# A second anchor for the first weight split of the GLU: ScalarE's half of it is ordered behind the last copy of the S5 loop's outputs

## The chip, the cores and the metric

The kernel runs on one core of a Trainium2 chip. The metric is device time in microseconds (us) of one execution. The core's engines are TensorE (PE in the profile, its weight loads PEld), VectorE (DVE), ScalarE (ACT), GpSimd (POOL) and SyncE (SP, which issues the DMAs). Each runs its own instructions in the order in which they were laid out, and waits on semaphores for the others.

## The reference, cut to what matters

Two layers of a residual network over 256 tokens of width 1024, then a second block. The place of interest is the mixer of the second layer: a bidirectional state-space recurrence (S5), a GELU, and a gated linear unit (GLU) with two 1024x1024 weight matrices.

```python
def _mixer_s5(h, lam_re, ..., d_skip, w_glu_a, w_glu_b):
    ...
    y = lax.map(one_sequence, ug).reshape(bsz, seq, dm)      # the S5 recurrence, both directions
    y = (y + d_skip.astype(f32) * u).astype(h.dtype)
    z = jax.nn.gelu(y)
    return (z @ w_glu_a) * jax.nn.sigmoid(z @ w_glu_b)
```

After it come the layer's feed-forward part, and a second block with three kinds of attention and a gated feed-forward part, nearly all of it dense products with float32 weights.

## The kernel before, in words

**Dense products.** A float32 weight tile of 1 MB is loaded by one DMA (`load`, L298) into one of four `w` buffers and split in four pieces by `hilo`: ScalarE writes the high part of a piece (`hi`, L314, 128x512), VectorE the rest (`lo`, L315). `mm3` (L319 to L321) then makes three matmuls for each block of 128: high weights by high activations, high weights by low activations, low weights by high activations. The same `hilo` splits activations.

**The S5 loop** (`s5`) runs over eight steps `ip`. In each, `chunk_states` multiplies the inputs by a table `Wt` on TensorE, ScalarE copies the result out of PSUM (the copy of `X`, L1047), TensorE transposes it (L1051), and `scan` works on it on VectorE: two products (L1064, L1065), a sum and a difference (L1066, L1067), the recurrence (L1068) and two products (L1072, L1073); GpSimd joins these into `S` (L1075, L1076). `outputs` multiplies the inputs by `Mt` (L1087) and `S` by `Vt` (L1089) into PSUM. Of every second step ScalarE copies the outputs to `Y` (L1122); the last of the four such copies is that of step 7. `chunk_states` runs one step ahead of `scan`. `X`, `S` and the two inputs of GpSimd share a ring of five buffers.

**The tail.** `finish(0)` and `finish(1)` handle the two halves of the channels. Each transposes its half of `Y` (L1099), adds the skip term on VectorE (L1102, eight instructions), takes the GELU on ScalarE (L1103) and splits the result in `z` high (L314) and low (L315), four pieces each. `finish(0)` needs only the steps 0 to 3, and its VectorE instructions are held behind the scan of step 7; `finish(1)` needs the last copy of `Y`.

**The GLU** (`j` = 0 to 3) loads and splits one tile of each matrix (`Wa`, `Wb`) and runs 48 matmuls for each, the even blocks first, which need only `finish(0)`, then the odd ones, which need `finish(1)`. Ahead of it `between` starts the preparation of the memory input `m` (squares L155, split L1230 and L1231); its ScalarE instructions are held behind the last one of `finish(1)`.

**What sets the order.** A planner lays the instructions of each engine out before the run, by the order of the code and by its own estimate of when inputs are ready; extra edges (`add_manual_dep`, set by `held` and `held_at`) tie it: an instruction that is emitted inside such a block is laid out behind the named one on its engine. `scanned` is such a set of anchors. It is made in each step and, after the loop, holds VectorE's last instruction of the scan of step 7. The split of the first GLU tiles (`j == 0`) is emitted inside `held_at(scanned)`, so VectorE's `lo` pieces come behind that scan. ScalarE's `hi` pieces and the loads have no anchor.

Of the kernel before, what the change touches and what calls it, by code (L numbers as in the profile page):

```python
# [174 lines left out]
class K:  # L175
# [784 lines left out]
    def s5(self, x, u, fill, need, between, each, l=1):  # L960
# [57 lines left out]
        def load(ip):  # L1018
            Wt = wide("Wt", self.wplace[ip], ip)
            Wt = [w.rearrange("p (e r d q) -> p e r d q", e=4, r=2, d=2) for w in Wt]  # L1020
            dm = tab([128, 2, 8, 32], "dm")
            if ip % 2 == 0:

                mt.append(room("Mt", self.mplace[ip // 2]).rearrange("p (a i e n) -> p a i e n", a=2, i=2, e=4))
                src = self.Kd[ip // 2]
                for s in range(8):
                    nc.sync.dma_start(mt[-1][16 * s:16 * s + 16].rearrange("c a i e n -> c (a i e) n"),
                                      bass.AP(tensor=src.tensor, offset=src.offset + 16 * s, ap=[[240, 16], [3840, 16], [1, 128]]))
            Mt = mt[-1][:, ip % 2]
            Et = self.E[:, :, 8 * ip:8 * ip + 8]  # L1030
            nc.gpsimd.memset(dm[:, :, :, 0], 0.0)
            (nc.scalar.copy if self.dm_act else nc.gpsimd.tensor_copy)(dm[:, :, :, 1:], self.rho[:, None, 8 * ip:8 * ip + 8, None].to_broadcast([128, 2, 8, 31]))
            Vt = wide("Vt", self.vplace[ip], ip)
            Vt = [w.rearrange("p (e r n) -> p e r n", e=4, r=2) for w in Vt]
            return Wt, Vt, Mt, Et[:, 0], Et[:, 1], dm

        def chunk_states(ip, tabs):

            Wt = tabs[0]
            pX = self.ps("mm").rearrange("p (i r d q) -> p i r d q", i=2, r=2, d=2)  # L1040
            for i in range(2):
                for d in range(2):
                    for e in range(4):
                        lhs = Ur[:, 2 * ip + i, e] if d else U[:, 2 * ip + i, 32 * e:32 * e + 32]
                        nc.tensor.matmul(pX[32 * e:32 * e + 32, i, :, d], lhs, Wt[i][:, e, :, d], start=True, stop=True, tile_position=(0, 32 * e))
            X = self.sb([128, 2, 2, 128])
            nc.scalar.copy(X, pX.rearrange("p i r d q -> p i r (d q)"))  # L1047
            pT = self.ps().rearrange("p (r i x) -> p r i x", r=2, i=2)
            for r in range(2):
                for i in range(2):  # L1050
                    nc.tensor.transpose(pT[:, r, i], X[:, i, r], self.ident)  # L1051
            return pT.rearrange("p r i (e j) -> p r (i e) j", e=4)
# [5 lines left out]
        def scan(pT, tabs):  # L1058
            cs, sn, dm = tabs[3:]
            both = lambda a: a[:, None].to_broadcast([128, 2] + list(a.shape[1:]))  # L1060

            t = [self.sb([128, 2, 8, 32], tag="q2") for _ in range(2)]
            a, b = t[0][:, :, :, 1:], t[1][:, :, :, 1:]
            tt(a, pT[:, :, :, 0:31], both(cs[:, :, 1:]), op=ALU.mult)  # L1064
            tt(b, pT[:, ::-1, :, 0:31], both(sn[:, :, 1:]), op=ALU.mult)  # L1065
            tt(Z[:, 0, :, 1:], a[:, 0], b[:, 0], op=ALU.add)  # L1066
            tt(Z[:, 1, :, 1:], a[:, 1], b[:, 1], op=ALU.subtract)  # L1067
            v.tensor_tensor_scan(fl(Tt), fl(dm), fl(Z), 0.0, op0=ALU.mult, op1=ALU.add)  # L1068
            S = self.sb([128, 2, 8, 32])
            fw, bw = slice(0, 64), slice(64, 128)  # L1070
            t = [self.sb([128, 2, 8, 32]) for _ in range(2)]
            tt(t[0], Tt, both(cs), op=ALU.mult)  # L1072
            tt(t[1], Tt[:, ::-1], both(sn), op=ALU.mult)  # L1073
            for r, op in ((0, ALU.subtract), (1, ALU.add)):
                nc.gpsimd.tensor_tensor(S[fw, r], t[0][fw, r], t[1][fw, r], op=op)  # L1075
                nc.gpsimd.tensor_tensor(S[bw, r, :, ::-1], t[0][bw, r], t[1][bw, r], op=op)  # L1076
            return S

        def outputs(ip, S, tabs, pY):
            _, Vt, Mt = tabs[:3]  # L1080
            for i in range(2):
                for k in range(3):
                    for e in range(4):
                        o = pY[32 * e:32 * e + 32, 2 * (ip % 2) + i]
                        kw = dict(start=k == 0, stop=k == 2, tile_position=(0, 32 * e))
                        if k == 0:
                            nc.tensor.matmul(o, U[:, 2 * ip + i, 32 * e:32 * e + 32], Mt[:, i, e], **kw)  # L1087
                        else:
                            nc.tensor.matmul(o, S[:, k - 1, 4 * i + e], Vt[i][:, e, k - 1], **kw)  # L1089

        def finish(ih):
            if ih == 0:
                z.extend(self.sb([128, 8, T], F32R, "h") for _ in range(2))
            zh, zl = z
            for t2 in range(2):
                po = self.ps("mm").rearrange("p (t e j) -> p t e j", t=4, e=4)
                for t in range(4):
                    src = Y[:, 4 * t2 + t, 8 * ih:8 * ih + 8].rearrange("p i c -> p (i c)")
                    nc.tensor.transpose(po[:, t].rearrange("p e j -> p (e j)"), src, self.ident)  # L1099
                for e in range(4):  # L1100
                    ut = u[:, ih, 4 * t2:4 * t2 + 4, e]
                    v.scalar_tensor_tensor(ut, ut, self.col("s5_d", 2 * e + ih), po[:, :, e], op0=ALU.mult, op1=ALU.add)  # L1102
            nc.scalar.activation(u[:, ih], u[:, ih], AF.Gelu_apprx_tanh)  # L1103
            for e in range(4):
                self.hilo(zh[:, 2 * e + ih].rearrange("p (t j) -> p t j", t=8), zl[:, 2 * e + ih].rearrange("p (t j) -> p t j", t=8), u[:, ih, :, e])
# [5 lines left out]
        for ip in range(8):  # L1111
            if ip + self.ahead < 8:
                tabs[ip + self.ahead] = load(ip + self.ahead)
            if ip + self.skew < 8:
                pT[ip + self.skew] = chunk_states(ip + self.skew, tabs[ip + self.skew])
            S = scan(pT.pop(ip), tabs[ip])
            scanned = {mybir.EngineType.DVE: self.last(mybir.EngineType.DVE)}
            if ip % 2 == 0:
                pY = self.ps(self.y_tag[ip // 2 % 2]).rearrange("p (i n) -> p i n", i=4)
            outputs(ip, S, tabs.pop(ip), pY)  # L1120
            if ip % 2:
                nc.scalar.copy(Y[:, :, 2 * ip - 2:2 * ip + 2].rearrange("p t i c -> p i t c"), pY.rearrange("p i (t c) -> p i t c", c=16))  # L1122
            if ip == 3 + self.defer:
                with self.held(mybir.EngineType.DVE):
                    finish(0)
            self.behind(fill, self.rates[2][1])
# [589 lines left out]
```

## Time and profile before

| | us |
|---|---|
| median of three runs | 1231.25 (1230.14 to 1233.12) |
| the profiled execution's own time | 1230.7 |
| its span on the core | 1228.9 |
| TensorE busy in the span | 1164.5 (95%) |
| VectorE busy | 888.7 (72%) |
| ScalarE busy | 610.8 (50%) |
| GpSimd busy | 97.4 (8%) |

The busy times are sums over stages with different limits; what ends last in a stage is read from its timeline. The times below are microseconds from the start of the span. TensorE's granted clock is a share of its full speed: 1.00 is 2.4 GHz, 0.50 is 1.2 GHz, and a value between is a mixture of the two within the stretch.

### The profile page before, as it was taken

The numbers are of one execution on the slowest core, as the hardware profiler recorded it, in microseconds if no ns is written. First come the engines' busy times: TensorE is split into PE (matmuls) and PEld (weight loads), VectorE is DVE, ScalarE is ACT, GpSimd is POOL, SyncE is SP. The second block draws the span as 40 slices with busy tenths as digits, with TensorE's granted clock in tenths as the row PEclk, the third lists the DMA queues.
The fourth block names the chain that finished last, engine by engine and source line by source line (L and its number), as shares of the span: only waits on it lengthen the run. The fifth ranks groups of instructions, "written<-read, shape, count | busy, mean of one in ns | idle before, by whom it ended". The sixth has DMA issues, their size and how long they took to land. (4 is left out here: it accounts for less than half of the span.)

```text
span 1228.9 us, 25406 instructions
## 1 busy us (share of the span) xinstructions
PE 1164.5 (95%) x10482; PEld 1104.8 (90%) x10482; DVE 888.7 (72%) x1827; ACT 610.8 (50%) x1202; POOL 97.4 (8%) x132
## 2 busy tenths in 40 slices
PE   5899898999999965899999999999999999999998
PEld 3698688999999953799999999999999999999998
DVE  7879888898989776857755656686666686665564
ACT  3577346555555542445544545563465545554441
POOL 0077310000000024200000000000000000000000
PEclk9799999999999976899999999999999999999999
DMA  9889786797988999354566655452444444555541
GB/s 341 326 315 331 300 319 203 242 308 276 312 290 273 272 279 294 142 174 169 176 240 217 225 176 181 151 175 101 144 166 138 167 167 151 194 180 177 193 154 60
DMA packets 69980, 267.29 MB, mean 218 GB/s; under 512 B 7381, under 2 KB 35429, under 8 KB 43241
## 3 DMA queue, kind: packets, MB, share of 16 engines
q1 hardware_dynamic: 69864, 265.68, 63.3%
q8 instruction: 82, 1.34, 0.4%
q14 instruction: 34, 0.27, 0.1%
HBM read 246.85 MB, written 18.81 MB: 216 GB/s over the span
## 5 line engine op out<-in xcount | busy, mean ns | idle before, releaser
L315 DVE TENSOR_TENSOR lo<-w,hi 128x512 fp32r<-128x512 f32 (+1 forms) x640 | 421.7, 702 | 142.5 <-ACT hi L314 142.0
L314 ACT ACTIVATE hi<-w 128x512 fp32r<-128x512 f32 (+1 forms) x640 | 358.1, 625 | 333.1 <-PE mm L320 117.4
L319 PE MATMUL mm<-h,hi 128*128 128x256 f32 x1328 | 381.5, 288 | 0.9 <-ACT hi L314 0.4
L321 PE MATMUL mm<-h,lo 128*128 128x256 f32 x1328 | 379.6, 286 | 0.1
L320 PE MATMUL mm<-h,hi 128*128 128x256 f32 x1328 | 378.6, 285 | 0.2 <-DVE h L384 0.2
L319 PEld LDWEIGHTS mm<-h,hi 128*128 128x128 f32 x1328 | 255.9, 193 | 8.7 <-issue 3.6
L321 PEld LDWEIGHTS mm<-h,lo 128*128 128x128 f32 x1328 | 255.8, 193 | 2.8 <-issue 1.5
L320 PEld LDWEIGHTS mm<-h,hi 128*128 128x128 f32 x1328 | 255.9, 193 | 1.3 <-issue 0.7
L320 PE MATMUL at<-s,hi 128*128 128x256 f32 x720 | 204.4, 284 | 0.0
L319 PE MATMUL at<-s,hi 128*128 128x256 f32 x720 | 204.4, 284 | 0.0
L321 PE MATMUL at<-s,lo 128*128 128x256 f32 x720 | 203.9, 284 | 0.0
L319 PEld LDWEIGHTS at<-s,hi 128*128 128x128 f32 x720 | 138.0, 192 | 1.8 <-issue 1.4
L320 PEld LDWEIGHTS at<-s,hi 128*128 128x128 f32 x720 | 138.0, 192 | 0.6 <-issue 0.6
L321 PEld LDWEIGHTS at<-s,lo 128*128 128x128 f32 x720 | 137.8, 192 | 0.4 <-issue 0.4
L443 PE MATMUL fa<-wa,crep 128*32 128x256 f32 x704 | 53.0, 418 | 8.0 <-DMA wa<-in_ada_dram 4.5
L541 POOL TENSOR_TENSOR s<-s,cv 128x256 f32<-128x256 f32 x60 | 50.1, 871 | 39.7 <-ACT cv L540 39.6
L443 PEld LDWEIGHTS fa<-wa,crep 128*32 128x32 f32 x704 | 20.7, 116 | 27.2 <-DMA wa<-in_ada_dram 6.7
L320 PE MATMUL fp<-h,hi 128*128 128x256 f32 x144 | 40.9, 284 | 1.6 <-DVE h L315 1.6
L319 PE MATMUL fp<-h,hi 128*128 128x256 f32 x144 | 40.8, 284 | 0.0
L321 PE MATMUL fp<-h,lo 128*128 128x256 f32 x144 | 40.7, 283 | 0.0
L540 ACT ACTIVATE cv<-ap,s 128x256 f32<-128x256 f32 x60 | 29.5, 505 | 17.4 <-POOL s L541 16.6
L937 ACT COPY Wt<-fp 128x512 f32<-128x512 f32 x32 | 18.6, 581 | 34.6 <-PE fp L936 28.0
(438 smaller groups left out, 1814.0 us busy)
## 6 DMA issues: line engine op xcount, KB each, us to landing
w<-in_fc_dram SPq DMA_DIRECT2D x64, 1024.0 KB, 5.1
wa<-in_ada_dram SPq DMA_DIRECT2D x44, 1024.0 KB, 6.5
w<-in_w_in_dram SPq DMA_DIRECT2D x38, 1024.0 KB, 4.9
w<-in_w_gate_dram SPq DMA_DIRECT2D x11, 1024.0 KB, 5.0
w<-in_w_up_dram SPq DMA_DIRECT2D x11, 1024.0 KB, 4.9
Vd<-V SPq DMA_DIRECT2D x16, 512.0 KB, 5.4
w<-in_w_out_dram SPq DMA_DIRECT2D x8, 1024.0 KB, 5.8
Wd<-Wt SPq DMA_DIRECT2D x16, 512.0 KB, 5.7
```

The costliest lines, as they stand in the source:

```text
L314: self.nc.scalar.activation(hi, h, AF.Copy)
L315: self.nc.vector.tensor_tensor(lo, h, hi.bitcast(F32), op=ALU.subtract)
L319: mm(ps, sh, mh, start=start, stop=False, skip_group_check=True)
L320: mm(ps, sh, ml, start=False, stop=False, skip_group_check=True)
L321: mm(ps, sl, mh, start=False, stop=stop, skip_group_check=True)
L443: nc.tensor.matmul(ps[32 * q:32 * q + 32], self.crep[:, 2 * k + k2], w[:, n:n + 256], start=k == 0 and k2 == 0, stop=k == 3 and k2 == 1, t ...
L540: nc.scalar.mul(t, src, w)
L541: nc.gpsimd.tensor_tensor(acc[:, ch], acc[:, ch], t, op=ALU.add)
L937: nc.scalar.copy(W[:, :, k], pt.rearrange("p (e x) -> p e x", e=4))
```

## The change

After the copy of `Y` in a step, the set of anchors gets a second entry: ScalarE's last instruction, which is that copy. At the end of the loop `scanned` so holds VectorE's last instruction of the scan and ScalarE's last copy of `Y`. The eight `hi` pieces of the first two GLU tiles are therefore laid out behind the last copy of `Y`. No instruction is added or removed, and no other edge changes.

```diff
             outputs(ip, S, tabs.pop(ip), pY)
             if ip % 2:
                 nc.scalar.copy(Y[:, :, 2 * ip - 2:2 * ip + 2].rearrange("p t i c -> p i t c"), pY.rearrange("p i (t c) -> p i t c", c=16))
+                scanned[mybir.EngineType.Activation] = self.last(mybir.EngineType.Activation)
             if ip == 3 + self.defer:
                 with self.held(mybir.EngineType.DVE):
                     finish(0)
```

## Rows read from the trace of the kernel before

**Rows 1.** Windows: stretch, length, busy us (instructions) per engine, granted clock, DMA share, GB/s

```profile
465.00:470.00 5.00, 4.92 (x76) 3.95 (x80) 2.68 (x5) 1.58 (x3) 0.15 (x2) 0.50 1.04 411
485.00:490.00 5.00, 0.00 (x0) 0.00 (x0) 0.00 (x0) 1.46 (x3) 0.00 (x0) 0.50 0.74 306
505.00:510.00 5.00, 3.38 (x28) 3.15 (x27) 4.93 (x15) 0.03 (x1) 0.00 (x0) 1.00 0.97 357
...
600.00:650.00 50.00, 50.00 (x421) 50.00 (x420) 31.33 (x53) 23.78 (x44) 0.00 (x0) 1.00 0.59 211
```

**Rows 2.** Waits of TensorE from 507 us on: total us, times, longest

```profile
PE fp L320 <- DVE h L315: 1.6, 1, 1.6
PE mm L320 <- DVE h L384: 0.2, 1, 0.2
```

**Rows 3.** Timeline of ScalarE: start, us, line, operation, [idle before <- releaser]

```profile
488.54 2.19 ACT L314 ACTIVATE hi<-w 128x512 fp32r<-128x512 f32 x4 [9.91 <-DMA w<-in_glu_b_dram]
490.64 0.56 ACT L1047 COPY s<-mm 128x512 f32<-128x512 f32 x1
491.10 2.19 ACT L314 ACTIVATE hi<-w 128x512 fp32r<-128x512 f32 x4
495.70 0.59 ACT L1122 COPY s<-at 128x512 f32<-128x512 f32 x1 [2.41 <-PE at L1089]
500.87 1.06 ACT L1103 ACTIVATE s<-s 128x1024 f32<-128x1024 f32 x1 [4.58 <-DVE s L1102]
501.95 1.33 ACT L314 ACTIVATE h<-s 128x256 fp32r<-128x256 f32 x4
503.56 0.59 ACT L1122 COPY s<-at 128x512 f32<-128x512 f32 x1 [0.27 <-PE at L1089]
509.97 1.06 ACT L1103 ACTIVATE s<-s 128x1024 f32<-128x1024 f32 x1 [5.82 <-DVE s L1102]
...
512.30 1.14 ACT L155 ACTIVATE q<-m 128x512 f32<-128x512 f32 x2
...
517.58 2.17 ACT L314 ACTIVATE hi<-w 128x512 fp32r<-128x512 f32 x4
```

**Rows 4.** Timeline of VectorE around the last scan and in the tail

```profile
481.56 1.23 DVE L1068 TENSOR_TENSOR_SCAN fp<-dm,fa 128x512 f32<-128x512 f32 x1
492.41 0.67 DVE L1064 TENSOR_TENSOR q<-at,E 128x496 f32<-128x496 f32 x1 [9.61 <-PE at L1051]
...
498.69 2.15 DVE L1102 SCALAR_TENSOR_TENSOR s<-s,vec,mm 128x128 f32<-128x128 f32 x8
500.75 5.77 DVE L315 TENSOR_TENSOR lo<-w,hi 128x512 fp32r<-128x512 f32 x8
506.44 1.42 DVE L315 TENSOR_TENSOR h<-s,h 128x256 fp32r<-128x256 f32 x4
507.79 2.14 DVE L1102 SCALAR_TENSOR_TENSOR s<-s,vec,mm 128x128 f32<-128x128 f32 x8
511.50 1.43 DVE L315 TENSOR_TENSOR h<-s,h 128x256 fp32r<-128x256 f32 x4 [1.57 <-ACT h L314]
```

**Rows 5.** Timeline of TensorE: end of step 7's chunk states, the hole, the GLU's start

```profile
473.34 0.27 PE L1045 MATMUL mm<-Wt,s 128*32 128x128 f32 x1
...
480.91 0.46 PE L1087 MATMUL at<-Vt,s 128*32 128x128 f32 x4 [0.81 <-issue]
491.25 1.12 PE L1051 MATMUL at<-ident,s 128*128 128x128 f32 x4 [9.88 <-ACT s L1047]
...
506.91 0.39 PE L320 MATMUL fp<-h,hi 128*128 128x256 f32 x1 [1.62 <-DVE h L315]
```

**Rows 6.** Timeline of GpSimd and of SyncE's queue: the issues that matter

```profile
478.03 0.73 POOL L1076 TENSOR_TENSOR s<-s,s 64x256 f32<-64x256 f32 x1
...
477.18 0.30 SPq L1027 DMA_DIRECT2D Mt<-Kd  x1
...
478.50 1.36 SPq L298 DMA_DIRECT2D w<-in_glu_a_dram  x1
```

**Rows 7.** DMA issues of narrow windows: size, us from issue to landing

```profile
Mt<-Kd SPq DMA_DIRECT2D x1, 128.0 KB, 6.5
...
w<-in_glu_a_dram SPq DMA_DIRECT2D x1, 1024.0 KB, 9.9
```

## The prediction

> **What bounds the kernel now.** I read the windows first, to find where TensorE is not full; then TensorE's waits behind the S5 loop; then the timelines of ScalarE, VectorE and TensorE between 473 and 518 us; last the landings of the transfers. In the windows the reader should see that from the GLU on TensorE has no hole: a stretch of 50 us holds 421 matmuls and is busy throughout [rows 1], and from 507 us to the end it waits on other engines twice, for 1.6 and 0.2 us [rows 2]. So whatever brings that stream forward brings the end forward, us for us, as long as the stream stays closed. The stream begins at 506.91, when the second GLU matmul gets its low activations [rows 5]. Ahead of it lies a hole: between 485 and 490 us TensorE, VectorE and GpSimd do nothing at all [rows 1].
>
> The timelines say whose hole it is. VectorE ends the recurrence of step 6 at 481.56 + 1.23 = 482.79 and then stands for 9.61 us until TensorE has transposed X of step 7; TensorE stands 9.88 us for ScalarE's copy of that X [rows 4, 5]. The product that the copy reads was done at 473.6 [rows 5]. The copy came at 490.64, because four `hi` pieces of the first GLU tile stood ahead of it on ScalarE, and these waited 9.91 us, from 478.63 on, for their weights [rows 3]. The tile was issued at 478.50 and took 9.9 us to land: 488.4, and the pieces start at 488.54 [rows 3, 6, 7]. The row names the other tile as the releaser, but this landing is the one that fits.
>
> **The change part by part.** Nothing is added or removed. Eight `hi` pieces move on ScalarE from either side of the copy of X of step 7 to behind the last copy of `Y`. Loads, SyncE and GpSimd keep their order.
>
> *The loop.* Without the pieces, X of step 7 still needs a buffer of the ring of five, which GpSimd frees when it ends `S` of step 4: 478.03 + 0.73 = 478.76 [rows 6]. With 0.56 us for the copy it is there at 479.4. TensorE is free at 480.91 + 0.46 = 481.37, and four transposes take at most 1.12, the figure at the low clock [rows 5]: 482.5 at the latest. VectorE is busy until 482.79. So its 9.61 us go, whole, and the rest of the loop moves up by 9.6 us.
>
> What is late next in the loop is the table `Mt` of steps 6 and 7: its last part is issued at 477.18 and lands 6.5 us later, at 483.7 [rows 6, 7]. TensorE's matmuls on it stand right behind the transposes, so TensorE waits about 1.2 us there with the outputs of step 5 queued behind. The copy of those outputs (495.70, so 486.1 when shifted) feeds only `finish(1)` [rows 3], and VectorE does not wait for it; I cost it at nothing. If the planner lays the `Mt` matmuls ahead of the transposes instead, VectorE waits until 483.7 + 0.6 + 1.1, some 2.6 us: that is the price if the cover is gone.
>
> *The tail.* Here the pieces now cost something. All of it 9.6 us earlier: the GELU of half 0 at 491.3, its high parts until 493.7, the last copy of `Y` from 493.96 to 494.55 [rows 3]. Then come the eight `hi` pieces, at 2.19/4 = 0.55 us each [rows 3]: until about 498.9. VectorE cannot start on the `lo` pieces at 491.2 as a mere shift of 500.75 would have it, but at about 495.1. It can use the gap for the low parts of half 0 (1.42 us, 492.9 to 494.3), which now stood behind the eight `lo` pieces. From 495.1 it has 5.77 (`lo`) + 2.14 (skip term of half 1) + 1.43 (low parts of half 1) = 9.34 us of work [rows 4], and is through at 504.5 at the earliest; shifted alone it would have been through at 511.50 + 1.43 - 9.6 = 503.3. So the tail gives back about 1.2 us.
>
> How this reaches TensorE depends on an order that the trace of before cannot show; I bound it from both sides. At 50/421 = 0.119 us per matmul [rows 1] the 96 matmuls of `j` = 0 take 11.4 us, 5.7 for the even blocks. Before, the odd blocks could start at 506.91 + 5.7 = 512.6, or 503.0 shifted. Worse end: VectorE makes all eight `lo` pieces first (to 500.9), then the skip term (503.0); GELU 1.06 and a first high part bring 504.5, and a first low part 504.8 [rows 3, 4]: 1.8 us late. Better end: the skip term first, as soon as the transposes of half 1 are done. Then the `lo` pieces come last, at 504.5, with only the last two blocks of one tile (1.4 us) and some backlog behind them: near 506.8, against 518.3 - 9.6 = 508.7: 1.9 us early. I take VectorE's own sum, +1.2, since VectorE is the engine that is full in this stretch (4.93 of 5 us [rows 1]).
>
> *Behind `j` = 0.* The loads of the next GLU tiles wait for `w` buffers that the `lo` pieces free, so they move with them. The later stream keeps its work. Since the planner lays out the rest anew, a hole the size of the largest one in the old stream, 1.6 us [rows 2], may come or not; I take zero, with that as its bound.
>
> Sum: -9.6 + 1.2 = -8.4 us. Against the profiled execution's own 1230.7 that is 1222.3; the median of before lies 0.55 above it, so 1222.8.
>
> **A rule weighed against the trace.** Between 465 and 470 us TensorE is busy for 4.92 us of 5 and yet has a granted clock of 0.50, the level of 1.2 GHz, after a thin stretch; in 505 to 510, after the thin tail, it has 1.00, that of 2.4 GHz [rows 1]. The Trainium skill (TensorE: Matmul & The Clock Gate, Part 1) says that the lower level is the default and that work lifts it. By that rule the GLU's first matmuls, now fed by VectorE at piece pace from about 495 us on, would run at the lower level; one of the two rows agrees and the other does not. It is a rival below, with a price from rows.
>
> **The rivals.**
>
> *The GLU begins at the low clock.* Stretches of both levels follow thin ones [rows 1]. If the even blocks of one tile (24 matmuls, 2.9 us) and some of the odd ones run at half speed, that adds 2.9 us at most; VectorE's feeding hides about a third. +2 us: 1224.8. Chance 0.10; before, the very same entry was at full clock.
>
> *Half of the `hi` pieces end up behind the memory input.* On ScalarE the GELU of half 1 comes up about 3.2 us after the last copy of `Y` (four transposes at 1.12 and the skip term at 2.14 [rows 4, 5]), when five or so pieces are made. The planner may then run GELU, high parts and all the work on `m` (512.30 to 517.58, 5.3 us [rows 3]) ahead of the other pieces, since that stands earlier in the code. Then ScalarE is through with half 1 at 500.5 and with `m` at 505.8; the second tile's first `lo` follows at 507.1, and its 48 matmuls (5.7 us) end at 512.9 against 508.7: 4.2 us of 9.6 lost, gain 5.4, 1225.8. For it: the code's order. Against: by the planner's own estimate the pieces were ready long before, or they would not have stood ahead of X. Chance 0.12.
>
> *Another wait takes the place of the old one in the loop.* If the copy of the outputs of steps 4 and 5 (L1122) is laid ahead of the copy of X, X waits for GpSimd's next `S` and for the matmuls on it, near 485; VectorE restarts near 487, and 4.2 us are lost: 1227. Chance 0.04.
>
> *Slower.* All eight pieces behind the GELU of half 1 and the work on `m`. Half 1 shifted is through at 512.30 - 9.6 = 502.7, `m` at 508.0, the first `hi` and `lo` at 509.4; the stream begins at 509.5 instead of 506.91, +2.6 us: 1233.9. It decides if the planner thinks the GLU weights land after the GELU of half 1 is ready, some 3 us behind the last copy of `Y`. Chance 0.07.
>
> *It doesn't do what it says.* X of step 7 stays where it was because something that I don't see holds it, and the time stays: 1231.2. Against it: the idle times of three engines lead back to the same four pieces, and the copy's input was ready 17 us earlier [rows 3 to 5]. Chance 0.07.
>
> **How the numbers follow.** The forecast has 0.60; its own range is a gain of 9.6 + 1.9 = 11.5 to 9.6 - 1.8 = 7.8: 1219.7 to 1223.5. A measurement of this kernel tells 0.2%, some 2.5 us, from no change. Faster by more than that are the forecast and the first three rivals: 0.60 + 0.10 + 0.12 + 0.04 = 0.86; the same 0.07; slower 0.07. The range of 8 in 10 takes in the forecast, the low clock, the half-delayed pieces and the other wait in the loop, but not no change: 1219.5 to 1227.5.
>
> **What would show it.** Right: no `hi` piece of a weight ahead of the copy of X of step 7, that copy near 479, VectorE's wait of 9.6 us before L1064 gone, the last copy of `Y` near 494, eight `hi` pieces behind it, and TensorE's closed stream from about 496 to 499 with at most a few us of holes. Wrong in its first step: VectorE again idle ahead of the scan of step 7, whatever the releaser. Wrong in its second: pieces of `m` on ScalarE between the `hi` pieces, or TensorE waiting on L315 of `lo` for more than 4 us. Wrong in its third: new waits of TensorE after 520 us, or a granted clock of 0.5 in the GLU's first us.

## The result and the profile after

The changed kernel takes 1221.7 us (median; 1220.8 to 1223.6) where the kernel before takes 1231.3: 9.6 us less, a ratio of 0.992 with a 95% interval of 0.9894 to 0.9945. The forecast was 1222.8 with a range of 1219.5 to 1227.5. Two more comparisons on other chips gave 8.2 and 9.4 us (below).

The profiled execution of the changed kernel took 1223.6 us, the slowest of its four runs, so its trace shows 7.1 us of gain, not 9.6; where the other 2.5 us lie comes out below. First ScalarE's timeline of the changed kernel, the counterpart of [rows 3] (start, us, line, operation, idle before and who ended it):

```profile
477.61 0.60 ACT L1032 COPY dm<-rho 128x496 f32<-128x496 f32 x1 [2.33 <-DVE fp L1068]
478.37 0.59 ACT L1047 COPY s<-mm 128x512 f32<-128x512 f32 x1 [0.16 <-POOL s L1076]
490.00 0.59 ACT L1122 COPY s<-at 128x512 f32<-128x512 f32 x1 [11.04 <-PE at L1089]
492.79 1.06 ACT L1103 ACTIVATE s<-s 128x1024 f32<-128x1024 f32 x1 [2.20 <-DVE s L1102]
493.88 1.34 ACT L314 ACTIVATE h<-s 128x256 fp32r<-128x256 f32 x4
495.13 0.59 ACT L1122 COPY s<-at 128x512 f32<-128x512 f32 x1
495.61 4.27 ACT L314 ACTIVATE hi<-w 128x512 fp32r<-128x512 f32 x8
500.27 1.06 ACT L1103 ACTIVATE s<-s 128x1024 f32<-128x1024 f32 x1 [0.39 <-DVE s L1102]
```

The copy of X of step 7 comes at 478.37, where it came at 490.64, and now waits 0.16 us for GpSimd, the releaser the prediction named. The eight pieces stand in one block behind the last copy of `Y`. VectorE's timeline, the counterpart of [rows 4]:

```profile
481.15 1.23 DVE L1068 TENSOR_TENSOR_SCAN fp<-dm,fa 128x512 f32<-128x512 f32 x1
482.28 0.66 DVE L1064 TENSOR_TENSOR q<-at,E 128x496 f32<-128x496 f32 x1
...
490.01 0.69 DVE L1073 TENSOR_TENSOR s<-fp,E 128x512 f32<-128x512 f32 x1 [1.98 <-PE at L1089]
490.61 2.15 DVE L1102 SCALAR_TENSOR_TENSOR s<-s,vec,mm 128x128 f32<-128x128 f32 x8
494.33 1.50 DVE L315 TENSOR_TENSOR h<-s,h 128x256 fp32r<-128x256 f32 x4 [1.57 <-ACT h L314]
496.28 1.29 DVE L315 TENSOR_TENSOR lo<-w,hi 128x512 fp32r<-128x512 f32 x2 [0.45 <-ACT hi L314]
497.49 1.11 DVE L1102 SCALAR_TENSOR_TENSOR s<-s,vec,mm 128x128 f32<-128x128 f32 x4
498.52 0.68 DVE L315 TENSOR_TENSOR lo<-w,hi 128x512 fp32r<-128x512 f32 x1
499.12 1.12 DVE L1102 SCALAR_TENSOR_TENSOR s<-s,vec,mm 128x128 f32<-128x128 f32 x4
500.16 3.09 DVE L315 TENSOR_TENSOR lo<-w,hi 128x512 fp32r<-128x512 f32 x5
503.17 1.42 DVE L315 TENSOR_TENSOR h<-s,h 128x256 fp32r<-128x256 f32 x4
```

From the start of the recurrence of step 6 to L1064 of step 7 it is 1.13 us, before 10.85: 9.7 us gone. But there is a wait of 1.98 us that was not there before, ahead of L1073 of step 7, and TensorE's timeline (the counterpart of [rows 5]) shows where it begins and what else was lost:

```profile
479.62 0.66 PE L1051 MATMUL at<-ident,s 128*128 128x128 f32 x4
485.94 0.66 PE L1087 MATMUL at<-Mt,s 128*32 128x128 f32 x8 [5.67 <-DMA m<-in_mem_dram]
...
488.86 1.08 PE L1089 MATMUL at<-h,s 128*32 128x128 f32 x16
...
498.38 0.58 PE L319 MATMUL fp<-h,hi 128*128 128x256 f32 x1 [1.51 <-ACT hi L314]
498.75 0.42 PE L320 MATMUL fp<-h,hi 128*128 128x256 f32 x1
498.97 0.41 PE L319 MATMUL mm<-h,hi 128*128 128x256 f32 x1
...
501.47 0.28 PE L319 MATMUL mm<-h,hi 128*128 128x256 f32 x1
501.59 0.28 PE L320 MATMUL mm<-h,hi 128*128 128x256 f32 x1
```

TensorE stands 5.67 us for the table `Mt` of steps 6 and 7. The row names another transfer, but the landing of the last part of `Mt` (issue, then us to landing) is the one that fits, at 485.6:

```profile
479.81 0.30 SPq L1027 DMA_DIRECT2D Mt<-Kd  x1
...
Mt<-Kd SPq DMA_DIRECT2D x1, 128.0 KB, 5.8
```

The outputs of step 5 are queued behind it and end at 488.86 + 1.08 = 489.94; L1073 starts at 490.01. The reading, tested below, is that they hold the buffer of `S` of step 5 and that L1073 needs it. Then the stream begins at 498.38, 8.5 us earlier than before, but its first 13 matmuls are 0.21 us apart instead of 0.12, the granted clock being 0.50. That gives back 13 x 0.095 = 1.2 us, and 7.3 are left, near the 7.1 by which the span is shorter. So of the 9.7 us the wait took 2.0 and the low clock 1.2. Some 0.4 was won ahead of the change, since the recurrence of step 6 began at 481.15 and not at 481.56, and 0.3 in the tail: 7.2. Behind the start of the stream nothing is lost: from 507 us on TensorE waits once.

```profile
PE mm L320 <- DVE h L384: 0.2, 1, 0.2
```

### The profile page after: what moved, and what is told of

Its sections match the earlier page's. It is cut to its first block, busy times and chain, and to the rows that moved or that the text cites. A ratio compares the mean times of both kernels' runs of the same rounds, so it can differ in the third digit from the quotient of the medians.

```text
span 1221.8 us, 25406 instructions
## 1 busy us (share of the span) xinstructions
PE 1164.1 (95%) x10482; PEld 1106.0 (91%) x10482; DVE 888.7 (73%) x1827; ACT 610.9 (50%) x1202; POOL 96.8 (8%) x132
```

## The experiments

**The theory.** The gain is the landing of the first GLU tile being taken out of the way of the copy of X; the place of the pieces behind the last copy of `Y` costs little; what the traces differ by is the late table and the clock at the GLU's entry. The rivals: the work or the place of the pieces matters, not the wait; or the order of the tail makes the gain. Four runs (half of the change, the anchor one place earlier, the anchor later, the sixth buffer) shared one chip, on which the kernel before took 1233.9 us, so they are read by their ratios to it.

**Half of the change.** Only the second tile's pieces get the anchor.

```diff
-                with self.held_at(scanned):
-                    Wa, Wb = self.piece("glu_a", j), self.piece("glu_b", j)
+                with self.held_at({mybir.EngineType.DVE: scanned[mybir.EngineType.DVE]}): Wa = self.piece("glu_a", j)
+                with self.held_at(scanned): Wb = self.piece("glu_b", j)
```

> Half of the change: only the second tile's four high pieces have the anchor behind the last copy of Y; the first tile's four stand ahead of the copy of X of step 7 as before the change. Theory: the stall is the wait of those first four for their weights, so it is all back: VectorE idle 9.6 us ahead of L1064 of step 7 and a time of 1229.5 to 1232.5. Rival: each tile's pieces cost half of the stall; then half of the gain stays: 1225 to 1228.

Measured: 1232.7 us, ratio 0.9989 (0.9973 to 1.0006): the whole gain is gone. ScalarE and VectorE in this kernel:

```profile
488.89 2.19 ACT L314 ACTIVATE hi<-w 128x512 fp32r<-128x512 f32 x4 [8.97 <-DMA w<-in_glu_b_dram]
490.98 0.56 ACT L1047 COPY s<-mm 128x512 f32<-128x512 f32 x1
...
492.75 0.68 DVE L1064 TENSOR_TENSOR q<-at,E 128x496 f32<-128x496 f32 x1 [8.66 <-PE at L1051]
```

Four pieces are enough for the stall, and it is back at 8.66 us. The other half, the first tile alone, was not run. This kernel's GLU begins at half clock, though its loop is the old one (window of 5 us: busy us per engine, granted clock, DMA share, GB/s):

```profile
505.00:510.00 5.00, 5.00 (x24) 5.00 (x25) 5.00 (x15) 2.18 (x5) 0.00 (x0) 0.50 0.89 329
```

**The pieces ahead of the copy, without their wait.** The kernel before, but the first tiles are split from the residual `x`, which is long on chip. The loads are still issued; the first quarter of the GLU is computed from `x` and not from its weights.

```diff
-                    Wa, Wb = self.piece("glu_a", j), self.piece("glu_b", j)
+                    Wa, Wb = (self.split((self.load(self.I[n][j][:, 0:8, :], 8, 256), x)[1], 8, 256) for n in ("glu_a", "glu_b"))
```

> The kernel before, with the first two GLU tiles' pieces split from a tile that has long been on chip (the residual x) and not from the loaded weights; the loads are still issued, and the GLU's first quarter is computed from x. No anchor for ScalarE: its pieces are laid out ahead of the copy of X of step 7, as before. Theory: the stall is the landing of the weights (488.4 us), not the place or the work of the pieces (4 x 0.55 us each); so with the pieces still ahead of the copy, VectorE's wait of 9.6 us shrinks to under 1 us and the time is that of the changed kernel, 7.5 to 11 us below before. Rival: pieces ahead of the copy cost by their place or their work; then 3 us or more of VectorE's wait stay and the time is at most 5 us below before.

Measured: 1221.6 us where before took 1231.3 on the same chip, ratio 0.9918 (0.9897 to 0.9939). ScalarE and VectorE:

```profile
468.06 2.19 ACT L314 ACTIVATE hi<-x 128x512 fp32r<-128x512 f32 x4 [0.95 <-PE at L1089]
...
476.57 2.19 ACT L314 ACTIVATE hi<-x 128x512 fp32r<-128x512 f32 x4
479.00 0.60 ACT L1032 COPY dm<-rho 128x496 f32<-128x496 f32 x1 [0.25 <-DVE fp L1068]
479.78 0.58 ACT L1047 COPY s<-mm 128x512 f32<-128x512 f32 x1 [0.17 <-POOL s L1076]
...
483.68 0.66 DVE L1064 TENSOR_TENSOR q<-at,E 128x496 f32<-128x496 f32 x1
```

All eight pieces stand ahead of the copy of X of step 7 and cost nothing that shows: they fill ScalarE's idle time, and the copy still waits for GpSimd's buffer. VectorE runs into L1064 without a wait. So it is the wait for the landing that made the stall, and not that the pieces stand ahead of the copy, nor their work. They stand further ahead of it than in the kernel before; pieces with their data there, right in front of the copy, were not run; an estimate from these rows is that they would hold it up by no more than their own 2.19 us. And this kernel has the old tail (eight low pieces ahead of the low parts of half 0) and by the medians is not slower than the changed one on its chip (1223.1): the new tail is no part of the gain that shows.

**The anchor one place earlier:** behind the copy of X of step 7.

```diff
-            nc.scalar.copy(X, pX.rearrange("p i r d q -> p i r (d q)"))
+            nc.scalar.copy(X, pX.rearrange("p i r d q -> p i r (d q)")); self.xcopy = self.last(mybir.EngineType.Activation)
...
-                scanned[mybir.EngineType.Activation] = self.last(mybir.EngineType.Activation)
+                scanned[mybir.EngineType.Activation] = self.xcopy
```

> The changed kernel with ScalarE's anchor one place earlier: the eight high pieces stand right behind the copy of X of step 7, no longer behind the last copy of Y. Theory: the gain is the copy of X getting ahead of the pieces, so the gain stays: copy of X near 478.5, VectorE's wait of 9.6 us ahead of L1064 gone, and the tail gets VectorE's old order (eight low pieces first). The pieces wait for their weights until about 488 to 493 and hold up the copy of the outputs of steps 4 and 5 and the GELU of half 0 by 0 to 2 us: 1220.5 to 1224. Rival: what counts is that the pieces are behind the last copy of Y (the order of the tail); then most of the gain is lost: 1228 to 1232.

Measured: 1225.0 us, ratio 0.9923 (0.99 to 0.9947): the gain stays. ScalarE:

```profile
490.56 2.19 ACT L314 ACTIVATE hi<-w 128x512 fp32r<-128x512 f32 x4 [10.30 <-DMA w<-in_glu_a_dram]
492.94 2.19 ACT L314 ACTIVATE hi<-w 128x512 fp32r<-128x512 f32 x4 [0.19 <-DMA w<-in_glu_b_dram]
495.03 0.56 ACT L1122 COPY s<-at 128x512 f32<-128x512 f32 x1
495.50 1.05 ACT L1103 ACTIVATE s<-s 128x1024 f32<-128x1024 f32 x1
```

The same wait for the weights is there again, 10.30 us on ScalarE, and now it holds up the copy of the outputs of steps 4 and 5 and the GELU of half 0. That GELU starts 5.06 us behind the first L1102 (490.44), where in the changed kernel it starts 2.18 us behind it: 2.9 us later, more than the 0 to 2 expected. By the ratios (0.9923 and 0.992) no loss shows, though the intervals reach some 3 us to either side. A wait of one length costs nearly ten microseconds ahead of one instruction and three at most, by this trace, ahead of the next.

**The anchor later:** behind the last ScalarE instruction of `finish(1)`. This is the slower rival of the prediction, made to happen.

```diff
-                scanned[mybir.EngineType.Activation] = self.last(mybir.EngineType.Activation)
...
         finish(1)
+        scanned[mybir.EngineType.Activation] = self.last(mybir.EngineType.Activation)
```

> The changed kernel with ScalarE's anchor later: behind the last ScalarE instruction of finish(1). The eight high pieces then stand behind the GELU of half 1 and behind two squares and the eight pieces of m. This is the slower rival of the prediction. By the sum over VectorE and ScalarE the pieces begin near 506.9 instead of 495.6, TensorE's GLU stream near 508.3 instead of 498.4; with all activations ready it then has no further holes: some 8 to 9.5 us lost against the changed kernel, 1229.5 to 1231.5. If the position in the tail were hidden by other work it would stay at 1222 to 1224.

Measured: 1228.2 us, ratio 0.9961 (0.9941 to 0.9981): by the ratio 4.8 us faster than before (5.7 by the medians), and by the ratios some 5 us slower than the changed kernel, not 8 to 9.5. ScalarE and TensorE:

```profile
502.16 3.29 ACT L1231 ACTIVATE mhh<-m,vec 128x256 fp32r<-128x256 f32 x8
505.35 4.26 ACT L314 ACTIVATE hi<-w 128x512 fp32r<-128x512 f32 x8
...
501.79 3.58 PE L167 MATMUL at<-inv,q 128*128 128x1 f32 x16 [4.79 <-ACT q L155]
506.02 0.58 PE L319 MATMUL mm<-h,hi 128*128 128x256 f32 x1 [0.65 <-ACT hi L314]
```

The layout is the one that the rival described, except that the pieces stand ahead of the last two squares of `m`. Half 1 is through earlier (501.2), since no low pieces stand in VectorE's way, and TensorE does the sums over `m` (16 matmuls, 1.84 us at full clock) in the hole, work that it else does inside the stream.

**The late table: a sixth buffer.** The changed kernel with one buffer more in the ring of X and `S`.

```diff
-        self.n2, self.nq, self.n1 = 5, 2, 8
+        self.n2, self.nq, self.n1 = 6, 2, 8
```

> The changed kernel with one more buffer in the ring that X, S and the two inputs of GpSimd share (six for five). In the trace after the change VectorE waits 1.98 us ahead of its last product of the loop (L1073), released by an outputs matmul (L1089). Theory: that wait is the ring: the product needs the buffer of S of step 5, which the outputs of step 5 hold, and these stand on TensorE behind the table Mt, which lands late. With six buffers the wait goes and the stream of the GLU comes up to 2 us earlier: 1219.7 to 1220.7. Rival: the late table holds the tail in any case, since the outputs of steps 5 to 7 queue behind it on TensorE: VectorE's wait goes, but the time stays within 0.5 us of 1221.7.

Measured: 1223.9 us, ratio 0.9918 (0.9897 to 0.9939), not to be told from the changed kernel's 0.992. The expected times were absolute and this chip was 2.5 us slower. By the ratios the theory's gain of 1 to 2 us over the changed kernel came out as 0.2, with intervals of some 3 us to either side: the time decides nothing between theory and rival. The trace (VectorE, then TensorE):

```profile
490.29 0.68 DVE L1073 TENSOR_TENSOR s<-fp,E 128x512 f32<-128x512 f32 x1
...
487.39 0.66 PE L1087 MATMUL at<-Mt,s 128*32 128x128 f32 x8 [3.55 <-DMA m<-in_mem_dram]
...
490.31 0.62 PE L1089 MATMUL at<-h,s 128*32 128x128 f32 x16
```

The table is late here too, and L1073 starts at 490.29 while the outputs of step 5 run until 490.93; with five buffers, in the changed kernel's first trace, it started only when they had ended. So the ring is the link, but a wait of 0.6 us is all that this execution had to show.

**The late table: its product last.** The outputs of steps 6 and 7 add the product with `Mt` behind the two with `Vt`.

```diff
-                for k in range(3):
+                for k in ((1, 2, 0) if ip > 5 else (0, 1, 2)):
...
-                        kw = dict(start=k == 0, stop=k == 2, tile_position=(0, 32 * e))
+                        kw = dict(start=k == (ip > 5), stop=k == (0 if ip > 5 else 2), tile_position=(0, 32 * e))
```

> The changed kernel in which the outputs of steps 6 and 7 add the product with the table Mt last and not first, so that TensorE no longer stands for the late table with the outputs of step 5 behind it. Theory: TensorE's wait of 3 to 5.7 us ahead of the Mt product goes, the buffer of S of step 5 comes free in time, VectorE's wait of 0.5 to 2 us ahead of L1073 of step 7 goes, as with a sixth buffer: 0.5 to 2 us faster than the changed kernel on this chip. Rival: the tail is bound by GpSimd's S of step 7 and what follows it in any case; VectorE's wait goes and the time stays within 0.5 us.

> The variant with the product with Mt added last, beside the changed kernel on one chip, since on the chip before it was 2.6 us faster by the medians with intervals that overlap. Theory: it takes away a wait that costs VectorE 0 to 2 us by the execution and brings the transposes of half 0 forward, so it is 0.5 to 2.5 us faster than the changed kernel. Rival: the difference was scatter between executions; then the medians lie within 0.5 us.

Beside them ran the changed kernel itself:

> The changed kernel once more, as the yardstick on this chip. In its first trace the GLU's first 13 matmuls ran at a granted clock of 0.50 (0.21 us apart for 0.12), which costs 13 x 0.095 = 1.2 us; before the change, the same entry ran at 1.00. Theory: the level at the entry is a matter of the execution, not of the change (of the five traces of the changed kernel and its variants, one entered at full clock and four at half; the half undo, whose loop is the old one, entered at half). Then this trace may show either, and the time stays 7 to 10 us below the kernel before. Rival: the change itself makes the entry slow; then every trace of this kernel shows 12 or more matmuls 0.21 us apart.

> The same changed kernel in another profiled execution, for the level of the clock at the GLU's entry. Theory as with the run before it: the level differs from execution to execution. Rival: always half.

> The changed kernel as the yardstick for the next run on one chip. Theory: 7.5 to 10 us below the kernel before (ratio 0.992 to 0.994), as on two other chips. Its trace shows once more whether the late table costs VectorE anything (0 to 2 us in the traces so far) and at which clock the GLU begins.

Measured, each pair on one chip:

| | before | changed | Mt last |
|---|---|---|---|
| first pair | 1231.3 | 1223.1 (1221.0 to 1224.1), ratio 0.9927 (0.991 to 0.9945) | 1220.5 (1219.9 to 1221.8), ratio 0.991 (0.9892 to 0.9929) |
| second pair | 1232.5 | 1223.1 (1221.8 to 1226.2), ratio 0.9929 (0.9904 to 0.9953) | 1222.2 (1220.8 to 1224.6), ratio 0.9919 (0.9897 to 0.9941) |

The variant is 2.6 and 0.9 us faster than the changed kernel by the medians, but the intervals overlap: a likely gain, not a shown one. What is shown is that the wait goes. TensorE's waits of the changed kernel in its four profiled executions (in the order first, second, third, fourth; total, times, longest):

```profile
PE at L1087 <- DMA m<-in_mem_dram: 5.7, 1, 5.7
```
```profile
PE at L1087 <- DMA m<-in_mem_dram: 1.6, 1, 1.6
```
```profile
PE at L1087 <- DMA m<-in_mem_dram: 3.1, 1, 3.1
```
```profile
PE at L1087 <- DMA m<-in_mem_dram: 5.6, 1, 5.6
```

Ahead of L1073 VectorE waited 1.98, 0, 0 and 1.88 us in them, and the GLU began at half clock in the first and fourth, at full clock in the second and third; those executions took 1223.6, 1223.1, 1221.1 and 1225.2 us. One at full clock and one at half (windows between 495 and 505 us: length, busy us per engine, granted clock, DMA share, GB/s; second execution, then fourth):

```profile
495.00:500.00 5.00, 2.78 (x46) 2.23 (x35) 4.47 (x12) 5.00 (x12) 0.00 (x0) 1.00 0.60 210
```
```profile
500.00:505.00 5.00, 4.36 (x21) 4.30 (x21) 5.00 (x14) 4.58 (x11) 0.00 (x0) 0.50 0.49 154
```

With the product last neither trace has the wait for `Mt` or that of VectorE, and from L1064 of step 7 to the first L1102 it takes 6.26 us in both, as in the better two of the changed kernel (6.25) and not as in the other two (8.3). One of the two still began the GLU at half clock, the other at full; so the clock is not bound to the late table.

These two terms do not make up the whole difference between the executions. The second and third have neither, and are 2.0 us apart, because the recurrence of step 6, ahead of all that was changed, began that much later in the second (second, then third):

```profile
483.96 1.23 DVE L1068 TENSOR_TENSOR_SCAN fp<-dm,fa 128x512 f32<-128x512 f32 x1
```
```profile
481.95 1.23 DVE L1068 TENSOR_TENSOR_SCAN fp<-dm,fa 128x512 f32<-128x512 f32 x1
```

Start of that recurrence, wait and clock together put the first execution 2.4 us behind the third, the second 2.0 and the fourth 4.8; measured were 2.5, 2.0 and 4.1. The two executions with the product last began the recurrence at 481.02 and 480.77, earlier than all four of the changed kernel (481.15 to 483.96), so a part of their lead in these traces stands ahead of what the variant changes. Where the differences ahead of the recurrence come from, no run shows.

## Why the prediction was right

**The loop** (9.6 us): right in its mechanism and size. Taking the wait away while the pieces stay ahead of the copy gives the whole gain, and leaving four waiting pieces ahead of the copy takes it all back.

**What is late next** (costed at nothing): the step that failed, by up to 2 us and not in every execution. The prediction saw that TensorE would wait for `Mt` with the outputs of step 5 behind it, and then followed only their copy to `Y`. It had named the ring of five buffers in the paragraph before, for X, and did not ask who else waits in it: `S` of step 5 is held until those outputs are done, and step 7's products need its place. It also took the landing of one execution (483.7) as fixed, 0.9 us after VectorE's L1064 of step 7 would begin; in the four traces TensorE's matmuls on the table began between 0.1 us ahead of L1064 and 3.7 us behind it. TensorE's wait, put at 1.2 us, was 1.6 to 5.7.

**The tail** (+1.2 us): the sign was wrong. From the first L1102 to the last low part of half 1 VectorE took 14.24 us before and takes 13.98 now, so the tail gives 0.3 us instead of costing 1.2. The eight low pieces were taken at 5.77 us; they take 1.29 + 0.68 + 3.09 = 5.06, because two of the eight had lasted 1.02 and 1.21 us before and none lasts over 0.70 now. The rest is that they start 5.7 us behind the first L1102, not 6.0, and that merged rows overlap a little. The order came out between the two bounds, skip term and low pieces in turns.

**Behind `j` = 0** (zero): right. From 507 us on TensorE waited once, for 0.2 us.

**The sum.** 9.7 us for the loop and 0.3 for the tail are 10.0, less 0 to 2 us for the table: 8 to 10. The clock takes up to 2 us in single executions, but the old loop can be struck as well (below), so it need not be in the difference of the medians. Measured: 9.6, 8.2 and 9.4 on three chips. The loop's term was reasoned; that the forecast of 8.4 came so close is in part luck, since two errors of opposite sign met: the tail, 1.5 us too dear, and the table, costed at nothing.

**The rivals.** The low clock at the entry was given 0.10 and came in two of four executions of the changed kernel, at 1.2 us (13 matmuls) and some 2.1 us (22 matmuls); it was priced at 2. A granted clock of 0.5 in the GLU's first us was also the prediction's own sign of being wrong in its third step. But the change is not needed for it: the half undo, with the old loop, began the GLU at half clock too. Whether the change makes it more frequent is open, with one trace of the kernel before. The prediction lacked that one and the same stretch can enter at either level. The Trainium skill (TensorE: Matmul & The Clock Gate, Part 1) says that the lower level is the default and that work lifts it; the two executions that began at 1.2 GHz agree, and the two that began at 2.4 GHz do not. The slower rival was priced at 1233.9, 2.6 us slower than before, and is wrong by more than 7 us: the kernel built for it is 4.8 us faster than before by the ratio. The prediction took the old times of half 1 and moved them by 9.6, with the low pieces still on VectorE ahead of it, and let TensorE begin only at the first low piece with the sums over `m` still to come. Half of the pieces behind `m` did not happen: all eight were laid out ahead of the GELU of half 1.

## What to carry to other kernels

An instruction whose input comes by DMA, laid out ahead of one on the critical chain, makes the whole chain wait for the transfer on an engine that runs in order, however little it does itself; look at the engines' idle time for a releaser that is a DMA, and ask what is queued behind it. Moving it was worth the whole stall here. Where to mattered little where what came behind had slack (one place earlier: no loss that shows), and took half of the gain where it had none (behind `finish(1)`: 4.8 us left). When a stall goes, follow every buffer that the next wait holds, not only the data.

## What the runs showed of the hardware

The same kernel enters a dense stretch at 1.2 or at 2.4 GHz from one execution to the next: in two of four traces the first 13 and 22 matmuls of the GLU were 0.21 us apart, in the other two 0.12. In a closed stream that goes straight into the time, 1.2 and some 2.1 us. The landing of the table (TensorE's wait for `Mt` was 1.6 to 5.7 us) cost VectorE 0 to 2 us, and the start of the recurrence of step 6 lay anywhere between 481.15 and 483.96 us: the three together make up the spread of some 4 us, to within 0.7, between the four profiled executions.

Two of the low pieces took 1.02 and 1.21 us in the kernel before where the other six took 0.68; they ran beside GpSimd's last two joins, of which the last took 1.08 us where its like took 0.72 (VectorE's first three pieces, then that join):

```profile
500.75 2.76 DVE L315 TENSOR_TENSOR lo<-w,hi 128x512 fp32r<-128x512 f32 x3
...
501.28 1.08 POOL L1076 TENSOR_TENSOR s<-s,s 64x256 f32<-64x256 f32 x1
```

In the kernel after, no join runs beside the pieces and all eight take 0.68 to 0.69. The Trainium skill (SBUF — State Buffer, Who interferes with whom) says that a VectorE instruction with two inputs in SBUF contends with a GpSimd instruction that reads SBUF; the trace agrees. A sum made from the old durations was too high by it.
